# Sum of reciprocals on one core: the last two rows as halves, another order for the last 48 rows, and other load sizes

## Chip, cores and metric

One core of a Trainium2 chip. The metric is the device time of one execution in microseconds (us). The kernel before takes 170.3 us in its fast state and 173.5 in a slow one that a good part of its executions fall into (29 of 64 in the last call); only fast runs are compared. A run counts as fast when it is at most 1.5% above the fastest of its kernel; a few runs of before near 172 us pass by this rule too (see below the table of runs).

## The reference

```python
x = np.abs(np.random.randn(32, 512, 1024)).astype(np.float32) + 1e-6
out = np.sum(1.0 / x, axis=-1)        # [32, 512]
```

That is 67.1 MB to read and 16,384 sums to write: 128 rows of 1024 elements on each of 128 partitions.

## The kernel before

A row's two halves a and b are taken together: 1/a + 1/b = (a + b) / (a b). The product a b comes from GpSimd (P in the list), or from VectorE (W from SBUF; V with one half copied by TensorE, C). ScalarE makes its reciprocal as exp(-ln(.)) (L, then E). VectorE multiplies and reduces it (R): over 1024 elements against both halves of the row, or over 512 where TensorE has added the halves into PSUM (S, two matmuls). The order of all this is a fixed list; each engine runs its own entries in order (the traces show all 153 operations of VectorE before the change, and all 151 after it, in the list's order by kind) and waits on semaphores. D8 loads the next eight rows into a ring of 40. P4+2 is two rows from row 4 on; the number behind @ is a PSUM bank or, for L, a slot for products. The traces record each of these matmuls as two, so a row's S shows there as four (268 records for 67 S in before's).

```python
    F = 128; R = 40; NP = 22          # rows, ring, slots for products
    PLAN = """
        D8 D8 D8 D8 D8 P0+2 C3@7 S2@0 V3 L0+2@0 P2 S3@1 E0+2@6 P4+2 S6@2 L2+2@2 R0 E2+2 R1
        ... (cut)
        S116@2 E112+2@6 R114 W117 L115+2@6 P118 R113 C119@5 E115+2 S119@0 R112 P120
        L117+2@14 V119 E117+2@6 S121@3 W121 R115 L119+3@8 P122 R118 S120@1 R117 E119+3 P123
        R116 S124@4 L122+2@20 P124 R121 R120 E122+2@6 W125 S125@2 R119 L124+2@11 P126 R123
        S126@0 E124+2 P127 R122 L126@3 R125 S127@1 E126 R124 L127@16 R126 E127 R127
    """.split()
    ...
            elif op == "R":
                other = ps[:, bank[r], :]
                if r in halves:                       # S has added the halves
                    row = prod[:, p, :]
                else:
                    row = ring[:, r % R, :].rearrange("p (h e) -> p h e", h=2)
                    other = other.unsqueeze(1).to_broadcast([P, 2, H])
                inst = nc.vector.tensor_tensor_reduce(
                    out=row, in0=row, in1=other, scale=S, scalar=0.0,
                    op0=mult, op1=add, accum_out=sums[:, r : r + 1])
```

## Time and profile before

| | before |
|---|---|
| first three times | 170.43, 170.23, 173.33 us |
| profiled run | 174.07 us, span 172.1 us, slow |
| data moved by DMA until | about 160.5 us, at some 425 GB/s |
| last load complete (all 16 increments) | 162.08 us |
| VectorE's last sum | 169.61 us |

The span runs from the first to the last instruction. An engine's busy time counts; what decides is the chain of waits that reaches the end. The lines are in the prediction below.

### The profile page before, as it was taken

Reading aid. Unit: us, or ns where it says so; the run is one execution under the profiler, and the core shown is the slowest. Engines: PE = TensorE matmul, PEld = TensorE weight load, DVE = VectorE, ACT = ScalarE, POOL = GpSimd, SP = SyncE. Lnnn points to the kernel's source line nnn. Section 1 sums busy time; section 2 is a strip of 40 time slices with the busy share of each in tenths; the row PEclk is TensorE's granted clock in tenths of the full one; section 3 lists DMA queues with packets and bytes.
Section 4 is the critical chain, followed back from the end, with each engine's and each line's share of the span. In section 5 each row is a group of like instructions: output and inputs, shape, how many; then the busy total and the mean of one; then the engine's idle time right before and its main releaser. Section 6 shows DMA issues by size and latency. Waiting matters only on the chain.

```text
span 172.1 us, 1294 instructions
## 1 busy us (share of the span) xinstructions
PE 136.1 (79%) x300; PEld 57.1 (33%) x300; DVE 131.9 (77%) x281; ACT 131.1 (76%) x133; POOL 124.6 (72%) x73
## 2 busy tenths in 40 slices
PE   0007999696987949489695999589999999997892
PEld 0003444242423424143342443134444343442440
DVE  0001786868689685868868689998699999999994
ACT  2002969979696977949698799989689796996992
POOL 1007969696997959589696999789739749977800
PEclk9999999999999999999999999969999999999999
DMA  6999999999999999999999999999999999999200
GB/s 198 427 442 411 449 411 449 411 449 427 449 421 396 427 434 430 421 442 411 434 428 430 404 426 447 424 426 429 427 416 423 429 424 413 410 410 409 101 0 15
DMA packets 4758, 67.24 MB, mean 391 GB/s; under 512 B 528, under 2 KB 656, under 8 KB 1808
## 3 DMA queue, kind: packets, MB, share of 16 engines
q1 hardware_dynamic: 4752, 67.18, 92.5%
q8 instruction: 2, 0.03, 0.1%
q14 instruction: 4, 0.03, 0.0%
HBM read 67.11 MB, written 0.07 MB: 390 GB/s over the span
## 4 chain that ended last, share of the span: by engine, by line
DMA 52%; DVE 29%; PE 6%; ACT 5%; issue 3%; POOL 3%; SPq 0%; ACTq 0%; POOLq 0%; DVEq 0%
DMA ring<-in_x_dram 52%; DVE ring L232 14%; DVE prod L232 8%; DVE prod L191 5%; PE ps L200 5%; POOL prod L175 3%; ACT ps L219 2%; ACT prod L210 2%; PE ps L185 1%; ACT prod L219 1%; DVE sums L232 1%; SPq L165 0%; ACTq L210 0%; POOLq L175 0%; DVEq L286 0%
## 5 line engine op out<-in xcount | busy, mean ns | idle before, releaser
L175 POOL TENSOR_TENSOR prod<-ring 128x1024 f32<-128x1024 f32 (+1 forms) x67 | 123.9, 1880 | 38.3 <-DMA ring<-in_x_dram 37.2
L200 PE MATMUL ps<-ring,ident 128*128 128x512 f32 x268 | 121.6, 606 | 5.2 <-DVE sums L232 2.6
L210 ACT ACTIVATE prod<-prod 128x1024 f32<-128x1024 f32 (+2 forms) x66 | 67.3, 1020 | 32.9 <-POOL prod L175 28.1
L232 DVE CUSTOM_DVE_ANT_1 ring<-ring,ps 128x1024 f32<-128x1024 f32 x61 | 72.1, 1216 | 17.9 <-ACT ps L219 17.9
L200 PEld LDWEIGHTS ps<-ring,ident 128*128 128x128 f32 x268 | 51.5, 194 | 73.7 <-issue 60.1
L232 DVE CUSTOM_DVE_ANT_0 prod<-prod,ps 128x512 f32<-128x512 f32 x67 | 43.4, 682 | 2.1 <-PE ps L200 1.6
L185 PE MATMUL ps<-ring,ident 128*128 128x512 f32 x32 | 17.9, 647 | 27.4 <-DMA ring<-in_x_dram 27.4
L219 ACT ACTIVATE prod<-prod 128x1024 f32<-128x1024 f32 (+2 forms) x34 | 35.4, 1042 | 0.9
L219 ACT ACTIVATE ps<-prod 128x1024 f32<-128x1024 f32 (+2 forms) x32 | 31.6, 986 | 3.2 <-DVE sums L232 2.4
L191 DVE TENSOR_TENSOR prod<-ring,ps 128x512 f32<-128x512 f32 x16 | 11.0, 685 | 17.7 <-PE ps L185 17.7
L185 PEld LDWEIGHTS ps<-ring,ident 128*128 128x128 f32 x32 | 5.6, 196 | 37.0 <-DMA ring<-in_x_dram 16.8
L232 DVE DVE_READ_ACCUMULATOR2_ANT sums<- 128x1 f32 x128 | 10.5, 82 | 0.0
L191 DVE TENSOR_TENSOR prod<-ring 128x512 f32<-128x512 f32 x9 | 10.2, 1154 | 0.0
L77 ACT ACT_TABLE_LOAD x1 | 1.3, 1283 | 0.7 <-PEq L275 0.7
masks.py:197 POOL MEMSET ident<- 128x128 f32 x1 | 0.2, 204 | 0.3 <-POOLq L275 0.3
masks.py:199 POOL TENSOR_SCALAR_AFFINE_SELECT ident<-ident 128x128 f32<-128x128 f32 x1 | 0.3, 292 | 0.1
L275 POOL MEMSET const-float32-0.0<- 128x1 f32 x1 | 0.1, 98 | 0.2 <-issue 0.2
L275 POOL MEMSET const-bfloat16-1.0<- 128x1 bf16 x1 | 0.1, 102 | 0.0
L275 POOL MEMSET const-uint8-127<- 128x1 uint8 x1 | 0.1, 102 | 0.0
L275 POOL MEMSET const-float32-1.0<- 128x1 f32 x1 | 0.1, 98 | 0.0
## 6 DMA issues: line engine op xcount, KB each, us to landing
ring<-in_x_dram SPq DMA_DIRECT2D x9, 4096.0 KB, 38.9
ring<-in_x_dram SPq DMA_DIRECT2D x7, 1536.0 KB, 35.5
ring<-in_x_dram SPq DMA_DIRECT2D x2, 2560.0 KB, 36.8
ring<-in_x_dram SPq DMA_DIRECT2D x9, 512.0 KB, 15.0
ring<-in_x_dram SPq DMA_DIRECT2D x1, 3072.0 KB, 36.4
ring<-in_x_dram SPq DMA_DIRECT2D x3, 1024.0 KB, 29.4
ring<-in_x_dram SPq DMA_DIRECT2D x1, 2048.0 KB, 36.8
out_dram<-sums SPq DMA_DIRECT2D x1, 64.0 KB, 1.5
```

Of the source, the lines that this page charges most:

```text
L77: nc.scalar.add_instruction(mybir.InstLoadActFuncSet(name=nc.get_next_instruction_name(), act_func_set_id=act_sets.index("natural_log_exp_ ...
L175: inst = nc.gpsimd.tensor_tensor(out=prod[:, p : p + m, :], in0=ring[:, a : a + m, :H], in1=ring[:, a : a + m, H:], op=mult,)
L185: inst = nc.tensor.matmul(ps[:, b, :], lhsT=ident, rhs=xs(r, 1), start=True, stop=True)
L191: inst = nc.vector.tensor_tensor(out=prod[:, p, :], in0=xs(r, 0), in1=in1, op=mult)
L200: inst = nc.tensor.matmul(ps[:, b, :], lhsT=ident, rhs=xs(r, h), start=h == 0, stop=h == 1,)
L210: inst = nc.scalar.activation(out=pg, in_=pg, func=Ln, scale=S)
L219: inst = nc.scalar.activation(out=rc, in_=pg, func=Exp, scale=-1.0)
L232: inst = nc.vector.tensor_tensor_reduce(out=row, in0=row, in1=other, scale=S, scalar=0.0, op0=mult, op1=add, accum_out=sums[:, r : r + 1],)
L275: nc = _bacc.Bacc("TRN2", target_bir_lowering=False, num_devices=1)
```

## The change

The intent is a shorter end: finer pieces for the last rows, an order of the last 48 rows found by a search that reckons with the overlap of ScalarE's operations (by before's trace, neighbours start 0.54 us apart where one lasts 0.63), and eight loads of 8 rows ahead of smaller ones. The early rows' order changes in places too.

```diff
+    LAST = F - 2
     PLAN = """  (all new; its end:)
+        ... W124 S123@0 L123@12 R122 L124@15 E123 W125 S125@1 E124@7 P126 R123 L125@16
+        R124 P127 L126@13 E125 P128 S128@0 L127@17 R125 E126@7 P129 S129@2 E127@6 R126
+        L128@18 L129@19 R127 E128 E129 R128 R129
     (loads: 9 of 8 rows and 23 more -> 8 of 8 rows, 25 more, 4 of half a row)
+    def place(r):                  # entries 126 to 129: halves of rows 126 and 127
+        if r < LAST:
+            return r, 0, H
+        q, part = divmod(r - LAST, 2)
+        return LAST + q, part * H, H // 2
 ... (P, C, V, W, S, L, E take width and place from it)
-                    scalar=0.0,
-                    accum_out=sums[:, r : r + 1],
+                    scalar=total if q in summed else 0.0,
+                    accum_out=total,            # total = sums[:, q : q + 1]
```

The second half of such a row starts its sum from the first half's, which it reads as a scalar operand.

More of the change, by code (lines that the diff above doesn't have):

```diff
@@ L25 @@
     NP = 22
+    LAST = F - 2
     S = float(2**17)
     PLAN = """
-        D8 D8 D8 D8 D8 P0+2 C3@7 S2@0 V3 L0+2@0 P2 S3@1 E0+2@6 P4+2 S6@2 L2+2@2 R0 E2+2 R1
-        S7@3 P6+2 L4+2@4 R2 R3 E4+2@6 L6+2@6 R4 P8+2 C11@5 E6+2 R5 D8 S10@0 V11 R6 L8+2@8
-        P10 S11@1 R7 E8+2@6 P12+2 S14@2 L10+2@10 R8 E10+2 R9 S15@3 P14+2 L12+2@12 R10 R11
-        E12+2@6 L14+2@14 R12 P16+2 C19@5 E14+2 R13 D8 S18@0 V19 R14 L16+2@16 P18 S19@1 R15
-        E16+2@6 P20+2 S22@2 L18+2@18 R16 E18+2 R17 S23@3 P22+2 L20+2@20 R18 R19 E20+2@6
@@ L39 @@
-        L22+2@0 R20 P24+2 C27@5 E22+2 R21 D8 S26@0 V27 R22 L24+2@2 P26 S27@1 R23 E24+2@6
-        P28+2 S30@2 L26+2@4 R24 E26+2 R25 S31@3 P30+2 L28+2@6 R26 R27 E28+2@6 L30+2@8 R28
-        E30+2 P32+2 C35@5 R29 D8 S34@0 V35 R30 R31 L32+2@10 P34 S35@1 E32+2@6 P36+2 S38@2
-        L34+2@12 R32 E34+2 R33 S39@3 P38+2 L36+2@14 R34 R35 E36+2@6 L38+2@16 R36 E38+2 R37
-        D6 P40+2 C43@6 R38 S42@0 R39 V43 L40+2@18 P42 S43@1 E40+2@6 P44+2 S46@2 L42+2@20 R40
-        E42+2 R41 D5 S47@3 P46+2 L44+2@0 R42 R43 E44+2@6 L46+2@2 R44 P48+2 C51@5 E46+2 R45
@@ L45 @@
-        D5 S50@0 V51 R46 L48+2@4 P50 S51@1 R47 E48+2@6 P52+2 S54@2 L50+2@6 R48 E50+2 R49
-        S55@3 P54+2 L52+2@8 R50 R51 E52+2@6 L54+2@10 R52 D5 P56+2 C59@5 E54+2 R53 D3 S58@0
-        V59 R54 L56+2@12 P58 S59@1 R55 E56+2@6 P60+2 S62@2 L58+2@14 R56 E58+2 R57 D4 S63@3
-        P62+2 L60+2@16 R58 R59 E60+2@6 L62+2@18 R60 P64+2 C67@5 E62+2 R61 D3 S66@0 V67 R62
-        L64+2@20 P66 S67@1 R63 E64+2@6 P68+2 S70@2 L66+2@0 R64 E66+2 R65 D3 S71@3 P70+2
-        L68+2@2 R66 R67 C75@7 E68+2@5 S74@0 P72+2 V75 L70+2@4 R68 D3 E70+2 S75@1 R69 D3
@@ L51 @@
-        L72+2@6 P74 R70 E72+2@6 R71 P76+2 L74+2@8 R72 S78@2 E74+2 R73 D3 P78+2 S79@3
-        L76+2@10 R74 R75 E76+2@6 C81@5 W82 L78+2@12 P80 R76 D2 L82@14 V81 E78+2 P85+3 S83@0
-        R77 D2 D1 E82@6 L80+2@15 R78 S87@1 R82 E80+2@4 R79 S84@2 L85+3@17 P83+2 R81 R80 D1
-        D1 D1 D1 D1 E85+3 S85@3 D1 P90 L83+2@20 R87 C91@7 R85 P92 L90@0 C88@6 V91 E83+2
-        S92@1 V88 P89 L91@3 R84 E90@7 R83 P94 S86@2 D1 D1 L88+2@4 R90 E91 W93 S93@0 E88+2@6
-        W95 R86 L92+2@1 R89 S91@2 E92+2 P96 R88 C99@7 R92 L94+3@6 P97+2 S99@3 R91 V99
@@ L57 @@
-        E94+3@4 R93 W100 S100@1 L97+2@9 P102 R94 L99+2@14 S101@0 R95 P101 E99+2 R96 S102@2
-        P103 L101+2@11 R100 R99 E97+2@6 P104+2 S105@1 L103@16 R97 E101+2 S104@3 R98
-        L104+2@20 P108 R101 E103@7 S107@4 W106 E104+2 W107 R103 L106+3@17 S106@0 P111 R105
-        E106+3 R104 S108@1 R102 P109+2 L111@13 R106 E111@7 R107 R108 C112@6 L109+2@4 P114
-        R111 S114@0 E109+2@4 V112 P113 L114@0 R109 S115@1 L112+2@1 P115 R110 E114 P116
-        S116@2 E112+2@6 R114 W117 L115+2@6 P118 R113 C119@5 E115+2 S119@0 R112 P120
@@ L63 @@
-        L117+2@14 V119 E117+2@6 S121@3 W121 R115 L119+3@8 P122 R118 S120@1 R117 E119+3 P123
-        R116 S124@4 L122+2@20 P124 R121 R120 E122+2@6 W125 S125@2 R119 L124+2@11 P126 R123
-        S126@0 E124+2 P127 R122 L126@3 R125 S127@1 E126 R124 L127@16 R126 E127 R127
+        D8 D8 D8 D8 D8 P0+2 C3@3 S2@0 V3 P2 L0+2@0 S3@1 E0+2@6 P4+2 S6@2 L2+2@2 R0 E2+2 R1
+        P6+2 L4+2@4 R2 R3 E4+2@6 S7@0 L6+2@6 R4 E6+2 P8+2 C11@3 R5 D8 S10@1 R6 R7 P10 L8+2@8
+        V11 S11@2 E8+2@6 P12+2 S14@0 L10+2@10 R8 E10+2 R9 P14+2 L12+2@12 R10 R11 E12+2@6
@@ new lines @@
+        S15@1 L14+2@14 R12 E14+2 P16+2 C19@3 R13 D8 S18@2 R14 R15 P18 L16+2@16 V19 S19@0
+        E16+2@6 P20+2 S22@1 L18+2@18 R16 E18+2 R17 P22+2 L20+2@20 R18 R19 E20+2@6 S23@2
+        L22+2@0 R20 E22+2 P24+2 C27@3 R21 D8 S26@0 R22 R23 P26 L24+2@2 V27 S27@1 E24+2@6
+        P28+2 S30@2 L26+2@4 R24 E26+2 R25 P30+2 L28+2@6 R26 R27 E28+2@6 S31@0 L30+2@8 R28
+        E30+2 R29 D6 P32+2 C35@3 S34@1 R30 R31 V35 P34 L32+2@10 S35@0 E32+2@6 P36+2 S38@2
+        L34+2@12 R32 E34+2 R33 D5 P38+2 L36+2@14 R34 R35 E36+2@6 S39@1 L38+2@16 R36 E38+2
@@ new lines @@
+        R37 D5 P40+2 C43@3 R38 S42@0 R39 V43 P42 L40+2@18 S43@1 E40+2@6 P44+2 S46@2 L42+2@20
+        R40 E42+2 R41 D3 P46+2 L44+2@0 R42 R43 E44+2@6 S47@0 L46+2@2 R44 E46+2 P48+2 C51@3
+        R45 S50@1 R46 R47 P50 L48+2@4 V51 S51@2 E48+2@6 P52+2 S54@0 L50+2@6 R48 D6 E50+2 R49
+        P54+2 L52+2@8 R50 R51 E52+2@6 S55@1 L54+2@10 R52 E54+2 P56+2 C59@3 R53 D5 S58@2 R54
+        R55 P58 L56+2@12 V59 S59@0 E56+2@6 P60+2 S62@1 L58+2@14 R56 E58+2 R57 D4 D2 P62+2
+        L60+2@16 R58 C67@3 R59 E60+2@6 S63@2 P64+2 V67 L62+2@18 R60 E62+2 S66@0 R61 D4 P66
@@ new lines @@
+        L64+2@20 R62 E64+2@6 R63 P68+2 S67@1 L66+2@0 R64 S70@2 E66+2 R65 D3 P70+2 L68+2@2
+        R66 R67 E68+2@6 S71@0 P72+2 L70+2@4 R68 D2 S74@1 E70+2 R69 D2 P74 L72+2@6 R70 C75@3
+        R71 E72+2@6 P76+2 S75@2 V75 R72 D2 L74+2@8 S78@0 R73 D2 D1 E74+2 P78+2 L76+2@10 R74
+        S80@3 R75 E76+2@6 P80 L78+2@12 S79@1 R76 D1 P81 L80@14 R77 D1 D1 D1 D1 E78+2 P82 E80
+        R78 R80 L81+2@15 R79 E81+2@6 P83 C88@5 R82 S85@0 P84 L83@17 R81 D1 D1 E83@7 P85
+        S86@1 L84@18 R83 D1 E84@6 P86 L85@19 V88 E85 R84 D1 D1 D1 D1 L88@21 P87 L86@20 R85
@@ new lines @@
+        C91@7 E88@6 P93 E86 R88 S90@0 L87@0 P92 E87@5 R86 R87 D1 D1 S89@1 P90 L92+2@1 V91
+        E92+2@5 W89 S91@2 P97 L89+3@3 R92 C94@7 R93 P95 L97@6 E89+3 S97@3 V94 P98 E97 R90
+        S98@4 P99 L98@9 R97 L94+2@7 R91 W96 S96@0 E98 R89 E94+2@6 R98 L96@14 R94 P100 C102@5
+        E96 S101@1 R96 P101 L99+2@10 R95 E99+2@3 P103 V102 L101@12 R99 C106@7 P104 L102+2@15
+        S104@0 R100 E101 P105 L104@13 R101 E102+2@5 S108@2 P107+2 V106 E104 R102 L105+2@17
+        S107@1 R104 E105+2@4 P109+2 R103 L107+2@19 R106 E107+2 R105 P111+2 S112@0 L109+2@0
@@ new lines @@
+        R107 E109+2@6 R108 S111@3 L111+2@2 W114 W113 S113@1 E111+2 R109 P115 L113@21 R111
+        P116 L114+2@4 S116@2 R112 E113 R110 P117 E114+2@5 S117@0 R113 P118 L116+2@6 R115
+        E116+2 P119 R114 L118@8 R116 P120 S120@1 L119@9 R117 E118@7 E119@6 R118 P121 L120@14
+        S121@0 E120 R119 P122 L121@10 S122@2 E121 R120 P123 L122@11 R121 E122 W124 S123@0
+        L123@12 R122 L124@15 E123 W125 S125@1 E124@7 P126 R123 L125@16 R124 P127 L126@13
+        E125 P128 S128@0 L127@17 R125 E126@7 P129 S129@2 E127@6 R126 L128@18 L129@19 R127
@@ L66 @@
+        E128 E129 R128 R129
     """.split()
@@ L104 @@
     pslot = {r + j: b + j for op, r, n, b in ops if op == "L" for j in range(n)}
+    def place(r):
[3 more added lines that the diff above has]
+        return LAST + q, part * H, H // 2
     def xs(r, h):
-        return ring[:, r % R, h * H : (h + 1) * H]
+        q, at, w = place(r)
+        return ring[:, q % R, at + h * w : at + (h + 1) * w]
     loaded = 0
-    bank, copied, halves = {}, {}, set()
+    bank, copied, halves, summed = {}, {}, set(), set()
     history = {}
@@ L149, in note, with rows @@
                 )
-    def rows(r, n):
-        return [("row", q % R) for q in range(r, r + n)]
+    def rows(r, n, h=None):
+        spaces = []
+        for q, at, w in (place(i) for i in range(r, r + n)):
+            end = at + 2 * w
+            if h is not None:
+                at, end = at + h * w, at + (h + 1) * w
+            spaces += [("row", q % R, i) for i in range(at, end, H // 2)]
+        return spaces
     def slots(r, n):
@@ L162 @@
                 while n:
-                    a = r % R
-                    m = min(n, R - a)
+                    q, at, w = place(r)
+                    a = q % R
+                    m = min(n, R - a, LAST - r) if r < LAST else 1
                     inst = nc.sync.dma_start(
-                        out=ring[:, a : a + m, :], in_=x_v[:, r : r + m, :]
+                        out=ring[:, a : a + m, at : at + 2 * w],
+                        in_=x_v[:, q : q + m, at : at + 2 * w],
                     )
@@ L172 @@
                 while n:
-                    a, p = r % R, pslot[r]
+                    q, at, w = place(r)
+                    a, p = q % R, pslot[r]
                     m = min(n, R - a)
                     inst = nc.gpsimd.tensor_tensor(
-                        out=prod[:, p : p + m, :],
-                        in0=ring[:, a : a + m, :H],
-                        in1=ring[:, a : a + m, H:],
+                        out=prod[:, p : p + m, :w],
+                        in0=ring[:, a : a + m, at : at + w],
+                        in1=ring[:, a : a + m, at + w : at + 2 * w],
                         op=mult,
@@ L185 @@
                 inst = nc.tensor.matmul(
-                    ps[:, b, :], lhsT=ident, rhs=xs(r, 1), start=True, stop=True
+                    ps[:, b, : place(r)[2]],
+                    lhsT=ident,
+                    rhs=xs(r, 1),
+                    start=True,
+                    stop=True,
                 )
-                note("PE", inst, rows(r, 1), [("bank", b)])
+                note("PE", inst, rows(r, 1, 1), [("bank", b)])
             elif op in "WV":
-                in1 = xs(r, 1) if op == "W" else ps[:, copied[r], :]
+                w = place(r)[2]
+                in1 = xs(r, 1) if op == "W" else ps[:, copied[r], :w]
                 inst = nc.vector.tensor_tensor(
-                    out=prod[:, p, :], in0=xs(r, 0), in1=in1, op=mult
+                    out=prod[:, p, :w], in0=xs(r, 0), in1=in1, op=mult
                 )
-                other = [("bank", copied[r])] if op == "V" else []
-                note("DVE", inst, rows(r, 1) + other, slots(r, 1))
+                if op == "W":
+                    read = rows(r, 1)
+                else:
+                    read = rows(r, 1, 0) + [("bank", copied[r])]
+                note("DVE", inst, read, slots(r, 1))
             elif op == "S":
@@ L200 @@
                     inst = nc.tensor.matmul(
-                        ps[:, b, :],
+                        ps[:, b, : place(r)[2]],
                         lhsT=ident,
@@ L206 @@
                     )
-                    note("PE", inst, rows(r, 1), [("bank", b)])
+                    note("PE", inst, rows(r, 1, h), [("bank", b)])
             elif op == "L":
-                pg = prod[:, p : p + n, :]
+                pg = prod[:, p : p + n, : place(r)[2]]
                 inst = nc.scalar.activation(out=pg, in_=pg, func=Ln, scale=S)
@@ L212 @@
             elif op == "E":
-                pg = prod[:, p : p + n, :]
+                pg = prod[:, p : p + n, : place(r)[2]]
                 rc = pg
                 if b is not None:
-                    rc = ps[:, b : b + n, :]
+                    rc = ps[:, b : b + n, : place(r)[2]]
                     for j in range(n):
@@ L225 @@
             elif op == "R":
-                other = ps[:, bank[r], :]
+                q, at, w = place(r)
+                other = ps[:, bank[r], :w]
                 if r in halves:
-                    row = prod[:, p, :]
+                    row = prod[:, p, :w]
                 else:
-                    row = ring[:, r % R, :].rearrange("p (h e) -> p h e", h=2)
-                    other = other.unsqueeze(1).to_broadcast([P, 2, H])
+                    row = ring[:, q % R, at : at + 2 * w]
+                    row = row.rearrange("p (h e) -> p h e", h=2)
+                    other = other.unsqueeze(1).to_broadcast([P, 2, w])
+                total = sums[:, q : q + 1]
                 inst = nc.vector.tensor_tensor_reduce(
@@ L236 @@
                     scale=S,
-                    scalar=0.0,
+                    scalar=total if q in summed else 0.0,
                     op0=mult,
                     op1=add,
-                    accum_out=sums[:, r : r + 1],
+                    accum_out=total,
                 )
+                summed.add(q)
                 note(
@@ L247 @@
                 )
-            elif op == "X":
-                row = ring[:, r % R, :]
-                inst = nc.scalar.activation(out=row, in_=row, func=Ln)
-                note("ACT", inst, writes=rows(r, 1))
-                inst = nc.scalar.activation(
-                    out=row,
-                    in_=row,
-                    func=Exp,
-                    scale=-1.0,
-                    accum_out=sums[:, r : r + 1],
-                )
-                note("ACT", inst, writes=rows(r, 1))
         nc.sync.dma_start(out=out_v, in_=sums)
```

## The prediction

> **What bounds the kernel now.** I read the page first for the spread of the load, then the busy time by stretch for the end of the run, then the chain that ended last, and then single durations and the timeline of the last 12 us. The page's strip of 40 slices (4.3 us each):
>
> ```profile
> PEclk9999999999999999999999999969999999999999
> DMA  6999999999999999999999999999999999999200
> GB/s 198 427 442 411 449 411 449 411 449 427 449 421 396 427 434 430 421 442 411 434 428 430 404 426 447 424 426 429 427 416 423 429 424 413 410 410 409 101 0 15
> ```
>
> The DMA engines are full from the second slice to slice 37 and move about 425 GB/s. So the 67.1 MB of x set the first 160 us, whatever the engines do, and only the way from the last load to the end can be shortened. One slice has a reduced TensorE clock. The stretches at the end:
>
> ```profile
> core 0: us, PE busy (x) PEld busy (x) DVE busy (x) ACT busy (x) POOL busy (x), PEclk, DMA share, GB/s
> ...
> 110.00:120.00 10.00, 7.42 (x14) 3.17 (x14) 9.60 (x18) 8.93 (x10) 7.84 (x4) 0.83 0.99 419
> ...
> 130.00:140.00 10.00, 9.65 (x23) 4.07 (x22) 10.00 (x23) 8.75 (x9) 8.41 (x6) 1.00 1.00 422
> 140.00:150.00 10.00, 9.61 (x23) 4.10 (x22) 9.84 (x21) 8.51 (x10) 7.94 (x6) 1.00 1.00 418
> ...
> 160.00:162.00 2.00, 2.00 (x6) 0.89 (x5) 2.00 (x5) 1.97 (x3) 1.18 (x2) 1.00 0.21 84
> 162.00:165.00 3.00, 3.00 (x9) 1.07 (x7) 3.00 (x10) 2.66 (x4) 1.44 (x2) 1.00 0.00 0
> 165.00:170.00 5.00, 3.64 (x9) 1.38 (x8) 4.61 (x12) 3.79 (x6) 0.00 (x0) 1.00 0.00 0
> ```
>
> From 130 us VectorE (DVE) has no gap, and data stop at about 160.5 us, yet VectorE works to 169.6. It carries a backlog of rows. The chain says where that came from:
>
> ```profile
> 112.55 0.14 issue
> 112.68 8.80 PE ps L200 x16
> 121.48 1.73 PE ps L185 x4
> 123.22 0.02 issue
> 123.24 0.69 DVE prod L191
> ```
>
> Sixteen matmuls took 8.80 us, 0.55 each, where the timeline elsewhere starts one every 0.43: in 113 to 117 us the granted clock was 0.57. That cost TensorE about 8.80 - 16 x 0.43 = 1.9 us, and VectorE never caught up. **This profile is a slow run** (174.07 us, against 170.43 and 170.23 of the fast ones), so its 7.5 us after the last load are not what fast runs have. That is the main point of what follows.
>
> [...] 1045 ns for 1024 elements and 620 for 512, and independent neighbours start 0.54 us apart where one lasts 0.63 (below, 167.07 and 167.61). [...] the VectorE product of two SBUF halves (W in the list) takes 1154 ns in the mean, that with a PSUM half (V) 685. [...] In the trace the last load's 16 increments spread from 159.87 to 162.08 us, so its row is usable 1.6 us after the bulk of the data.
>
> **The change part by part.** Durations come from these groups by shape:
>
> ```profile
> L175 POOL TENSOR_TENSOR prod<-ring 128x1024 f32<-128x1024 f32 x34 | 80.6, 2386 | 25.7 <-DMA ring<-in_x_dram 25.7
> L232 DVE CUSTOM_DVE_ANT_1 ring<-ring,ps 128x1024 f32<-128x1024 f32 x61 | 72.1, 1216 | 17.9 <-ACT ps L219 17.9
> L232 DVE CUSTOM_DVE_ANT_0 prod<-prod,ps 128x512 f32<-128x512 f32 x67 | 43.4, 682 | 2.1 <-PE ps L200 1.6
> L175 POOL TENSOR_TENSOR prod<-ring 128x512 f32<-128x512 f32 x32 | 40.9, 1293 | 10.7 <-DMA ring<-in_x_dram 9.6 <-ACT ps L219 1.0
> L191 DVE TENSOR_TENSOR prod<-ring 128x512 f32<-128x512 f32 x9 | 10.2, 1154 | 0.0
> L210 ACT ACTIVATE prod<-prod 128x512 f32<-128x512 f32 x8 | 5.0, 620 | 1.8 <-DVE prod L191 1.8
> ```
>
> In a row back to back they overlap: in the chain a reduction over 1024 elements takes 1.14 us, one over 512 takes 0.60, and a free product 0.60.
>
> *Loads.* By the times at which the loads' semaphores fill, eight rows land every 9.70 us, three every 3.69, one every 1.275: about 1.205 us per row plus 0.07 per load. The list goes from 32 to 37 loads (nine of 8 rows become eight, nine of one row become eleven, and the last two rows become four of half a row). So the last landing moves by 5 x 0.07 = 0.35, from 162.08 to 162.43. Row 125 lands at 159.74 and the halves at 160.41, 161.09, 161.76 and 162.43. Loads stay requested several microseconds ahead, so nothing starves.
>
> *VectorE, rows from 80 on.* Before: 27 short and 21 long reductions, 6 V, 9 W: 27 x 0.60 + 21 x 1.14 + 6 x 0.60 + 9 x 1.154 = 54.1 us. After: 23 short, 23 long, two over 512 and two over 256 elements (estimate 0.35 from the slope), 5 V, 6 W: 13.8 + 26.2 + 1.2 + 0.7 + 3.0 + 6.9 = 51.8. That is 2.3 us less, but in 60 us of loads, so only a backlog would turn it into time.
>
> *The end before, in a fast run.* Two floors. Last row: landed 162.08, product to 163.43, logarithm 0.61, exponential 0.63, reduction 0.69 and 0.1 of hand-over: 165.5. VectorE: W121 cannot start before row 121 is there, 154.50, and behind it come W125, nine short and four long reductions: 2 x 0.60 + 9 x 0.605 + 4 x 1.14 = 11.2, so 165.8 with 0.1 of waking. The slow profile ended VectorE at 169.6; the fast runs are 174.07 - 170.43 = 3.64 shorter, so about 166.0. **Fast runs already sit on the floor of 165.8**: the backlog that the profile shows is that of a slow run.
>
> *The end after.* VectorE floor: W125 from 159.84, then R123 0.605, R124 1.14, R125 0.605, R126 and R127 0.60 each, R128 and R129 0.35 each: with W125's own 0.60 that is 4.85, so 164.7. Last half: GpSimd takes about 0.75 for half a row (line through 1284 at 512 and 2386 at 1024 elements). It runs P126 from 160.5 to 161.25, P127 to 162.0, P128 to 162.75, and P129, whose half landed at 162.43, to 163.5. Then L129, E128 and E129 of 0.40 each, the two exponentials overlapping by 0.1 beside each other, to 164.6, then R129 0.35 and a hand-over: about 165.1. Against 166.0 that is **0.85 us less**.
>
> How the tail of before looked in the profile, ScalarE:
>
> ```profile
> 167.07 0.63 ACT L219 ACTIVATE prod<-prod 128x512 f32<-128x512 f32 x1
> 167.61 0.61 ACT L210 ACTIVATE prod<-prod 128x512 f32<-128x512 f32 x1
> 168.25 0.63 ACT L219 ACTIVATE prod<-prod 128x512 f32<-128x512 f32 x1
> ```
>
> *ScalarE and list.* Single rows replace pairs and threes from row 80 (50 operations of 512 or 256 elements instead of 16). Each costs 0.2 more than its share of a pair, and interleaving rows gives back 0.09 per neighbour. Sum for rows from 80: 2 x (21 x 0.615 + 4 x 0.40 + 11 x 1.045 + 1.48) = 55 us, less some 4 of overlap, in 60 us of loads: it fits, with little to spare. The early rows' new order and the loads' sizes there lie under the full DMA.
>
> Sum: 170.43 - 0.85 = 169.6 us.
>
> **Rivals.** (1) *The backlog is real in fast runs too.* Then the 2.3 us less of VectorE work and the finer end are worth up to the distance from 169.6 to 165.1, and the time is 166 to 168. For it: the unbroken VectorE busy time. Against it: fast runs are 3.6 us shorter than the profiled one, and the backlog follows a clock dip. (2) *A new wait takes the gain.* VectorE runs in order, and W124 and W125 stand in its list waiting for loads [...]. The last two reductions also read the sum that the one before them writes. ScalarE's single operations leave it little slack. Then 170.4 to 171.2. (3) *DMA loses more on 2 KB pieces than on 4 KB ones*: if a half takes 0.75 instead of 0.67, 0.3 us of the gain goes, 169.9. (4) *Transfers hide it all*: the early part of the change should do nothing, as its rows wait for data.
>
> **Range and chances.** From the step of 0.85 less, plus or minus rival 2 or half of rival 1: 168.4 to 170.8. Faster by over 2% needs under 167.0, another 2.6 us, more than the whole VectorE saving, or rival 1 in full: 4%. Slower by over 2% needs 3.4 us of new waits: 3%. Within 2%: 93%.
>
> **What would show it.** In the profile after: the last load's semaphore full about 0.35 us later than before, if the DMA runs alike; half-row products near 0.75 us and half-row ScalarE operations near 0.40; six W with a mean near or under 1.15; the output issued under 3.2 us after the last landing. It is wrong if VectorE is still busy without a gap for over 4 us after the last landing in a run with full clock (rival 1 or 2), or if the stretch from 150 us moves under 395 GB/s (rival 3). If the profile after falls in the fast state, it says little against a slow one: then the timed runs decide.

The 1045 and 620 ns are ScalarE's operations over 1024 and 512 elements (L210 in before's profile). The last row's product on GpSimd started at 162.15 us, 0.07 after the last of the 16 increments.

## The result, and the profile after

A ratio is the mean time of one kernel's fast runs over that of the other's in the same rounds, so not quite the ratio of the medians quoted. After: 170.06 us median (169.95 to 170.29, four runs), ratio to before 0.9986, interval 0.9962 to 1.001. Two later comparisons gave 0.9981 (0.9972 to 0.9991) and 0.9970 (0.9950 to 0.9989). So it is about 0.3 us faster in the fast state, not 0.85.

The stretches of the changed kernel's end, busy time by engine (columns as in the prediction):

```profile
160.00:162.00 2.00, 2.00 (x7) 1.01 (x6) 1.75 (x4) 2.00 (x5) 1.86 (x3) 1.00 0.17 65
162.00:165.00 3.00, 1.61 (x8) 1.08 (x6) 2.47 (x10) 2.09 (x7) 0.93 (x2) 1.00 0.00 0
165.00:170.00 5.00, 0.00 (x0) 0.00 (x0) 0.49 (x2) 0.00 (x0) 0.00 (x0) 0.60 0.06 16
```

No engine is full after 162 us, and VectorE ends at 165.65; the last load was complete at 161.88. Nothing has a backlog, and still 3.77 us pass. VectorE's timeline there:

```profile
163.29 0.08 DVE L264 DVE_READ_ACCUMULATOR2_ANT sums<- 128x1 f32 x1
163.53 0.75 DVE L264 CUSTOM_DVE_ANT_1 ring<-ring,ps,sums 128x512 f32<-128x512 f32 x1 [0.15 <-DVE sums L264]
164.20 0.08 DVE L264 DVE_READ_ACCUMULATOR2_ANT sums<- 128x1 f32 x1
164.20 0.42 DVE L264 CUSTOM_DVE_ANT_0 prod<-prod,ps 128x256 f32<-128x256 f32 x1
164.54 0.08 DVE L264 DVE_READ_ACCUMULATOR2_ANT sums<- 128x1 f32 x1
165.17 0.48 DVE L264 CUSTOM_DVE_ANT_0 prod<-prod,ps,sums 128x256 f32<-128x256 f32 x1 [0.54 <-DVE sums L264]
165.57 0.08 DVE L264 DVE_READ_ACCUMULATOR2_ANT sums<- 128x1 f32 x1
```

These are R127, R128 and R129 with the reads that store their sums. R127 and R129 take a sum as operand (the name `sums` behind the arrow), and VectorE waits for itself: 0.15 and 0.54 us (0.15 to 0.16 and 0.54 to 0.55 in two more profiles of this kernel and in a_pause). Why the second wait is the longer is open: R127 starts 0.10 us after VectorE's own semaphore instruction, R129 0.46 us after it, though ScalarE's last exponential had ended at 164.20. The new short operations, from the groups by shape:

```profile
L217 DVE TENSOR_TENSOR prod<-ring 128x512 f32<-128x512 f32 x6 | 4.0, 688 | 0.4 <-DMA ring<-in_x_dram 0.4
L196 POOL TENSOR_TENSOR prod<-ring 128x256 f32<-128x256 f32 x4 | 2.8, 726 | 1.9 <-DVE prod L217 1.9
L239 ACT ACTIVATE prod<-prod 128x256 f32<-128x256 f32 x4 | 1.5, 404 | 0.0
```

They cost what was reckoned (0.75 and 0.40). The six W take 688 ns, where before's nine take 1154 in its slow profile and 824 in its fast one (below). They hardly meet GpSimd's products any more: one starts in the last 0.12 us of such a product (691 ns), the others beside none. In before's slow profile the five W that start inside one take 1.00 to 1.85 us, the other four 0.68 to 0.69.

### The profile page after: what moved, and what is told of

Read it like the earlier page. It is cut to its first block, busy times and chain, and to the rows that moved or that the text cites. A ratio compares the mean times of both kernels' runs of the same rounds, so it can differ in the third digit from the quotient of the medians.

```text
span 168.3 us, 1338 instructions
## 1 busy us (share of the span) xinstructions
PE 131.5 (78%) x290; PEld 54.2 (32%) x290; DVE 128.3 (76%) x281; ACT 133.3 (79%) x155; POOL 129.4 (77%) x82
## 4 chain that ended last, share of the span: by engine, by line
DMA 72%; DVE 8%; POOL 6%; PE 4%; issue 4%; ACT 3%; SPq 0%; DVEq 0%; POOLq 0%
DMA ring<-in_x_dram 72%; POOL prod L196 6%; DVE ring L264 4%; PE ps L229 4%; DVE prod L264 2%; ACT ps L248 2%; ACT prod L239 1%; DVE prod L217 1%; DVE sums L264 0%; SPq L184 0%; DVEq L264 0%; POOLq L196 0%; DVEq L307 0%
## 5 line engine op out<-in xcount | busy, mean ns | idle before, releaser
L196 POOL TENSOR_TENSOR prod<-ring 128x1024 f32<-128x1024 f32 (+2 forms) x76 | 128.7, 1726 | 33.0 <-DMA ring<-in_x_dram 30.6
L229 PE MATMUL ps<-ring,ident 128*128 128x512 f32 (+1 forms) x260 | 117.0, 598 | 10.1 <-DVE sums L264 8.9
L239 ACT ACTIVATE prod<-prod 128x1024 f32<-128x1024 f32 (+2 forms) x77 | 68.7, 902 | 28.3 <-POOL prod L196 27.6
L264 DVE CUSTOM_DVE_ANT_1 ring<-ring,ps 128x1024 f32<-128x1024 f32 x64 | 75.4, 1209 | 19.4 <-ACT ps L248 19.0
L229 PEld LDWEIGHTS ps<-ring,ident 128*128 128x128 f32 x260 | 49.4, 193 | 76.4 <-issue 54.6
L264 DVE CUSTOM_DVE_ANT_0 prod<-prod,ps 128x512 f32<-128x512 f32 x64 | 41.5, 678 | 0.8 <-ACT prod L248 0.4
L248 ACT ACTIVATE prod<-prod 128x1024 f32<-128x1024 f32 (+3 forms) x40 | 35.0, 881 | 0.9
L206 PE MATMUL ps<-ring,ident 128*128 128x512 f32 x30 | 17.5, 667 | 22.0 <-DMA ring<-in_x_dram 21.6
L248 ACT ACTIVATE ps<-prod 128x1024 f32<-128x1024 f32 (+2 forms) x37 | 33.5, 908 | 1.0
L217 DVE TENSOR_TENSOR prod<-ring,ps 128x512 f32<-128x512 f32 x15 | 10.2, 683 | 16.1 <-PE ps L206 15.9
L206 PEld LDWEIGHTS ps<-ring,ident 128*128 128x128 f32 x30 | 4.8, 196 | 32.6 <-issue 14.4
L217 DVE TENSOR_TENSOR prod<-ring 128x512 f32<-128x512 f32 x6 | 4.0, 688 | 0.4 <-DMA ring<-in_x_dram 0.4
```

What stands on the lines that cost most here:

```text
L196: inst = nc.gpsimd.tensor_tensor(out=prod[:, p : p + m, :w], in0=ring[:, a : a + m, at : at + w], in1=ring[:, a : a + m, at + w : at + 2 * w],
L206: inst = nc.tensor.matmul(ps[:, b, : place(r)[2]], lhsT=ident, rhs=xs(r, 1), start=True, stop=True,)
L217: inst = nc.vector.tensor_tensor(out=prod[:, p, :w], in0=xs(r, 0), in1=in1, op=mult)
L229: inst = nc.tensor.matmul(ps[:, b, : place(r)[2]], lhsT=ident, rhs=xs(r, h), start=h == 0, stop=h == 1,)
L239: inst = nc.scalar.activation(out=pg, in_=pg, func=Ln, scale=S)
L248: inst = nc.scalar.activation(out=rc, in_=pg, func=Exp, scale=-1.0)
```

## The experiments

Theory A: the sum of a second half must wait until the first half's sum is stored, and this chain on VectorE ate the gain. Rivals: the end hangs on ScalarE or GpSimd (B), the halves as such carry the gain (C), reading a sum costs at any distance (D). The first call had b_again to a_whole, the second a_nochain2 to b_halved, the third a_whole3 to a_inter_few, the last the rest.

| run | median us of all runs | fast runs | ratio to before (interval) |
|---|---|---|---|
| b_again | 173.50 | 1 of 6 | none given |
| a_again | 170.09 | 16 of 16 | 0.9981 (0.9972 to 0.9991) |
| a_nochain (wrong on purpose) | 168.41 | 6 of 6 | 0.9881 (0.9859 to 0.9904) |
| a_nochain2 (wrong on purpose) | 169.41 | 6 of 6 | 0.9913 (0.9867 to 0.9960) |
| a_inter | 169.92 | 6 of 6 | 0.9940 (0.9893 to 0.9986) |
| a_whole2 | 171.18 | 6 of 6 | 1.0016 (0.9970 to 1.0063) |
| b_halved | 174.96 | 2 of 6 | 1.0063 (0.9970 to 1.0157) |
| a_whole3 | 170.74 | 22 of 22 | 1.0009 (0.9991 to 1.0026) |
| a_inter38 | 169.51 | 15 of 15 | 0.9940 (0.9917 to 0.9963) |
| a_loads34 | 176.73 | 6 of 6 | 1.0342 (1.0294 to 1.0391) |
| a_inter_few | 175.37 | 6 of 6 | 1.0283 (1.0235 to 1.0331) |
| b_again2 | 170.54 | 14 of 20 | 1.0000 (0.9970 to 1.0030) |
| a_pause | 170.46 | 22 of 22 | 0.9985 (0.9969 to 1.0002) |
| a_again2 | 170.05 | 22 of 22 | 0.9970 (0.9950 to 0.9989) |
| a_inter38b | 169.47 | 11 of 11 | 0.9928 (0.9904 to 0.9953) |

The runs of before near 172 us that count as fast (2 of 7 in the second call, 5 of 30 in the third, 3 of 35 in the last, none in the first) pull these ratios down. Worked out again without them, a_inter has 0.9970, a_inter38b 0.9943, a_again2 0.9980.

**The same two kernels again** (no edit).

> The kernel before, unchanged, to get a profile of it in the fast state and the noise of the comparison. Theory of the record: VectorE ends at about 166.0 us and the last load is complete at 162.0, so fast runs sit on their floor. Rival: the last load lands earlier in fast runs (161.5 or less) and some backlog of VectorE stays. Ratio to before 1.000 within 0.002.

> The changed kernel, unchanged, beside the same runs of before as the others of this call: ratio 0.9986 within 0.002 if the first comparison holds; 0.995 if the forecast of 0.85 us less was right and the first four runs were unlucky.

a_again repeated the result; b_again's profile was slow again, with the half clock at 113 us (a granted clock of 0.83 over 110 to 120 us, as in before, whose trace has 0.50 from 113.42 to 116.84).

**Without the chain.** Both kernels give each half a sum column of its own:

```diff
-    sums = pool.tile([P, F], f32)
+    sums = pool.tile([P, COLS], f32)          # COLS = F + 2
-                total = sums[:, q : q + 1]
+                total = sums[:, r : r + 1]
-                    scalar=total if q in summed else 0.0,
+                    scalar=0.0,
-        nc.sync.dma_start(out=out_v, in_=sums)
+        nc.sync.dma_start(out=out_v, in_=sums[:, :F])      # a_nochain
+        nc.sync.dma_start(out=out_v, in_=sums[:, 2:COLS])  # a_nochain2
```

> The changed kernel, but each half of the last two rows has a sum column of its own, so no reduction reads the sum that the one before it wrote. Wrong on purpose: rows 126 and 127 of each partition get one half's sum alone. Theory A (chained sums cost the gain: 0.15 + 0.07 us at R127 and 0.54 + 0.06 at R129): VectorE ends about 0.7 to 0.9 us earlier than in the changed kernel, 169.2 us, ratio to before 0.994. Rival B (the end hangs on ScalarE or GpSimd and the wait lies beside it): within 0.1 us of the changed kernel.

> As a_nochain, but the output waits for all four half sums (in a_nochain it took columns 0 to 127 and left 0.6 us before the last two reductions ended, so its time flattered). Wrong on purpose: the columns put out are 2 to 129. Theory A (chained sums cost about 0.95 us on VectorE, from R126's start to the last read of a sum 2.97 against 2.01 us): 169.1 us, ratio to before 0.9925. Rival B': the gain of a_nochain was only the early output: 170.0.

a_nochain gained more than theory A allows: its output was issued at 163.81 us, before the last two reductions had ended. That was a fault of the experiment. a_nochain2 mends it: 169.41, where A said 169.1 and B' 170.0. On VectorE, from R126's start to the last stored sum, 2.97 us became 2.01. So B falls.

**The halves in another order, correct.**

```diff
-        q, part = divmod(r - LAST, 2)
+        part, q = divmod(r - LAST, 2)
```

The entries are now 126a, 127a, 126b, 127b, so one other reduction stands between writing and reading a sum. One of the four loads moved behind R87, which frees its place.

> The changed kernel, correct, with the four halves in another order: first halves of rows 126 and 127, then their second halves, so that a reduction reads a sum that the one before the last wrote. Theory A: most of the 0.95 us comes back, 169.2 to 169.5 us, ratio 0.993 to 0.995. Rival D (it is the read of a sum as scalar operand itself that costs, at any distance): still 170.0.

VectorE's end in a_inter, by the timeline:

```profile
163.90 0.48 DVE L264 CUSTOM_DVE_ANT_0 prod<-prod,ps,sums 128x256 f32<-128x256 f32 x1
164.31 0.08 DVE L264 DVE_READ_ACCUMULATOR2_ANT sums<- 128x1 f32 x1
164.31 0.48 DVE L264 CUSTOM_DVE_ANT_0 prod<-prod,ps,sums 128x256 f32<-128x256 f32 x1
164.71 0.08 DVE L264 DVE_READ_ACCUMULATOR2_ANT sums<- 128x1 f32 x1
```

Both second halves read a sum and neither waits. The last load was complete at 161.88 as in the changed kernel, and VectorE ended at 164.79 instead of 165.65: 0.86 us, as theory A said. D falls: from R126's start it is 2.13 us, 0.12 above the version that reads no sum. But the time fell by 0.14 only (medians on two chips; the two profiled runs, 170.09 and 169.76 us, differ by 0.33).

**Where the other 0.7 us went.** The first step is at the very end. After issuing the output, SyncE goes through some waits and joins the other engines. In a_inter its trace (the packed one, as no view lists these instructions) has a pause of 0.41 us between its 79th and 80th recorded instruction, where such neighbours stand 0.04 to 0.06 apart; a_whole2 has 0.41 at the same place. In the changed kernel the 79th and 80th enclose the wait for the output itself (1.18 us), so a pause there would be hidden. a_inter's stream is one instruction shorter. Two runs test it. a_inter38 (and a_inter38b, the same file) splits one load of two rows, so the stream grows by two:

```diff
-        ... D2 L74+2@8 S78@0 R73 D2 D1 E74+2 ...
+        ... D2 L74+2@8 S78@0 R73 D1 D1 D1 E74+2 ...      (and a_inter's edit)
```

a_pause loads the second half of each of the two rows first, which needs one wait less and shortens the changed kernel's stream by one; its work is otherwise the same, and it is correct:

```diff
-        return LAST + q, part * H, H // 2
+        return LAST + q, (1 - part) * H, H // 2
```

> a_inter with its last load of two rows split into two loads, 38 loads in all. In a_inter VectorE ended 0.86 us earlier than in the changed kernel, the time fell by 0.14 only. Its SyncE pauses 0.41 us between its 79th and 80th instruction, and there the output is already complete; in the changed kernel the same place in the stream falls into the wait for the output. Theory P (a pause at a fixed place of the instruction stream): one more load moves the place into the wait; the span shrinks by 0.37 less 0.07 for the load: 169.6 us. Rival: the pause stays behind the output or another comes: 169.9 to 170.0.

> The changed kernel with the second half of each of the two last rows loaded first. The work is the same, instruction by instruction; one load needs one semaphore less, so SyncE's stream is one instruction shorter (86 for 87) and the place of its pause falls just behind the completed output. Theory P: VectorE ends as in the changed kernel, 165.6 to 165.8, and the time is 0.35 us longer: 170.4. Rival: 170.05 as the changed kernel.

> The changed kernel as it is, on the same chip as a_pause and a_inter38b: 170.05 to 170.10 us, ratio to before 0.998.

> a_inter38 once more, the candidate that beats both kernels, on the same chip as the changed kernel: 169.5 us, 0.55 less than a_again2, ratio to before 0.994 to 0.995. Rival: the first call had a quick chip, and the two are within 0.2 us.

On one chip: a_again2 170.10 in the mean, a_pause 170.47 (its VectorE ended at 165.49, and the pause of 0.41 stood behind the output), a_inter38b 169.47 (the pause of 0.43 stood ahead of the wait for the output, inside the transfer). The times are as expected, though a_pause's VectorE ended a little before the 165.6 of its expectation and a_inter38b's ratio fell below its 0.994. So the pause is worth about 0.37 us when it is exposed. That it belongs to a place in SyncE's stream is shown by seven traces at four lengths of the stream (82, 84, 86 and 88 instructions), all with the pause between the 79th and the 80th; what SyncE does there is open. It had taken about 0.4 of a_inter's gain. In the two profiled runs the account closes: SyncE passes the wait for the output at 166.57 instead of 167.34, 0.77 earlier (the transfer took 0.09 longer), and needs 1.37 us instead of 0.97 behind it, so the span is 0.37 shorter. That the medians differ by 0.14 only has no run of its own; profiled single runs of one kernel differ by as much as 0.4 (168.3 and 168.7 us of span for the changed one).

a_inter38 beats both kernels: 0.63 us less than the changed one on the same chip, 0.7% less than before (0.6% without the runs near 172 us).

**The last rows whole, with the new list.** a_whole was spoilt: the two loads left out were the wrong ones, so a row was overwritten before it was read (215.83 us, wrong result); nothing follows from it. a_whole2 and a_whole3 are correct. They differ in whether TensorE adds the halves of row 126:

```diff
-    LAST = F - 2
+    LAST = F
 ... (two of the four D1 taken out; the end of the list:)
-        P128 S128@0 L127@17 R125 E126@7 P129 S129@2 E127@6 R126 L128@18 L129@19 R127 E128 E129 R128 R129
+        S126@0 E125 L126@13 R125 S127@2 E126 L127@17 R126 E127 R127        # a_whole2
+        L126@13 E125 R125 E126@6 S127@0 L127@17 R126 E127 R127            # a_whole3
```

> The changed list and loads, but the last two rows whole, as before. Theory A: a whole last row needs 1.28 + 0.61 + 0.63 + 0.69 us behind its landing at 161.85, so VectorE ends at about 165.3 to 165.5, which is the same as or a little better than the changed kernel's 165.65: the halves gain nothing as they are. Rival C (the halves are what makes the changed kernel the faster): 0.5 to 1.2 us slower than it, above 170.5.

> The changed list and loads with whole last rows, as a_whole should have been: there the two loads left out were the wrong ones, so row 127 was loaded before row 87 had been read, and the result was wrong and the run meaningless. Theory A: VectorE ends at 165.3 to 165.5, so 169.8 to 170.1 us: the halves gain nothing as they are. Rival C (the halves make the changed kernel what it is): above 170.6.

> The changed list with whole last rows once more; in a_whole2 both whole rows were summed on TensorE, whose 20 matmuls in a row ended only at 165.25 us and set the end. Here row 126 goes without TensorE (a long reduction), row 127 with it, as of the four halves two go each way. If TensorE's queue alone made whole rows slower: VectorE ends at 165.2 to 165.5 and the time is 170.0 to 170.4 (with the pause of SyncE of 0.37 us that a_whole2 and a_inter show after the output). If halving the last row's latency is worth something by itself: VectorE ends at 165.9 or later, above 170.5.

a_whole2's expectation missed. Its last line on the timeline of VectorE says why:

```profile
165.40 0.69 DVE L263 CUSTOM_DVE_ANT_0 prod<-prod,ps 128x512 f32<-128x512 f32 x1 [1.02 <-PE ps L228]
```

R127 waited for TensorE, whose queue of twenty recorded matmuls ended that late: S126 and S127 over 512 elements had replaced S128 and S129 over 256. That was a choice of the experiment. In a_whole3 row 126 goes without TensorE: VectorE ends at 165.68, as in the changed kernel (165.65), and the 170.76 us of its fast runs' mean holds an exposed pause of 0.41. Less that pause it is 170.4. This expectation missed too: VectorE's end lies between its two cases, and the time is where rival C put it. But in the profiles the output is complete at 167.27, in the changed kernel at 167.34, and SyncE then needs 1.61 us instead of 0.97: the pause, and waits that it passed before the output's end in the changed kernel. So the time lost lies wholly behind the output, and on VectorE rival C falls for the change as it stands: the halves gain nothing there, and a_nochain2 and a_inter show that the chain takes what they save. With the chain loosened (a_inter) they are worth 0.86 to 0.89 us there.

**The old list with halves.** The end of before's list, halves spliced in, in the changed kernel's code:

```diff
-        W125 S125@2 R119 L124+2@11 P126 R123 S126@0 E124+2 P127 R122 L126@3 R125 S127@1 E126 R124 L127@16 R126 E127 R127
+        W125 S125@2 R119 L124+2@11 P126 R123 E124+2 P127 R122 L126@3 R125 P128 S128@0 L127@13 E126@7 R124 P129
+        S129@1 E127@6 R126 L128@18 L129@19 R127 E128 E129 R128 R129
```

> The list and loads of before, with only the last two rows as halves. Theory A (VectorE's backlog from W121 on is the floor of before, and the halves add about 0.7 us of reductions and 0.9 us of waits behind it): slower than before by 0.7 to 1.6 us, 171.0 to 171.9 in the fast state. Rival C (halves shorten the last row and that is what counts): 0.5 us or more faster than before.

Only two runs were fast, 171.61 and 172.36, beside fast runs of before with a median of 170.44. The direction is that of theory A, but the interval reaches below 1, so this alone decides nothing. No profile of it is fast.

**Larger loads.** The changed list with nine loads of 8 rows and larger ones behind them, each issued as soon as its rows are free; a_inter_few does the like with a_inter and 33 loads.

```diff
-    8 x D8, D6, D5, D5, D3, D6, D5, D4, D2, D4, D3, D2 D2 D2 D2, 11 x D1, 4 halves      (37 loads)
+    9 x D8, D6, D5, D5, D5, D3, D4, D3 D3 D3 D3 D3, D2 D2, 7 x D1, 4 halves             (34, a_loads34)
+    9 x D8, D6, D5 D5 D5 D5 D5, D4, D3 D3, D2 D2, 9 x D1, 4 halves                      (33, a_inter_few)
```

In both, one of the loads of 5 rows crosses the end of the ring and is cut in two, as one of before's is; the 34 of a_loads34 counts it, the 33 of a_inter_few does not.

> The changed kernel with nine loads of 8 rows and before's sizes behind them: 34 loads for 37, each issued as soon as its rows are free. If the size of a load costs 0.07 us each, the last half lands 0.2 us earlier and VectorE ends 0.1 to 0.2 us earlier; if the end hangs on TensorE and VectorE alone, no change of VectorE's end (165.65). By the count of its waits SyncE's pause falls behind the output: time 169.9 to 170.4.

> The candidate: a_inter with 33 loads (nine of 8 rows, larger ones after them), so that the last half lands about 0.2 us earlier and SyncE's stream ends before its 79th instruction. Expected 169.2 to 169.6 us, ratio to before 0.993 to 0.996. If bursts of larger loads make rows wait: 170 or more.

Both are over 5 us slower than the kernels that they were made from. Of what was expected, only a_inter_few's other case (170 or more, if bursts make rows wait) has the direction, and neither has the size. Their last loads landed as early as ever (161.54 and 161.66). The stretches of a_loads34, then the same of the changed kernel:

```profile
90.00:100.00 10.00, 7.87 (x15) 3.44 (x16) 7.23 (x16) 7.68 (x8) 8.55 (x5) 0.83 0.97 412
...
120.00:130.00 10.00, 10.00 (x20) 4.19 (x19) 8.08 (x16) 7.25 (x10) 7.03 (x6) 0.81 1.00 424
...
160.00:165.00 5.00, 3.73 (x9) 1.67 (x10) 5.00 (x14) 4.78 (x9) 2.54 (x4) 1.00 0.03 13
```

```profile
90.00:100.00 10.00, 9.59 (x21) 3.93 (x22) 9.07 (x22) 9.84 (x11) 10.00 (x6) 1.00 0.99 424
...
120.00:130.00 10.00, 10.00 (x25) 4.49 (x24) 9.43 (x20) 9.45 (x12) 8.17 (x7) 1.00 1.01 424
```

The data flow alike (the last two columns), but in 90 to 130 us VectorE does 32.2 us of work (with the two stretches not shown) instead of 36.4, and then has no gap from 140 to 165. Rows that arrive in larger bursts leave the list, tuned to other arrivals, waiting: ahead of its V, VectorE waited 21.0 us in all for TensorE's copies, 15.9 in the changed kernel, and row 72 lands at 99.31 instead of 96.09. Half clocks at 93 and 117 us (granted 0.83 over 90 to 100 us, 0.85 and 0.81 over the two stretches from 110 us) come on top, and the six W of a_loads34 take 1014 ns in the mean again, and no run tells the two shares apart.

**Before in the fast state.**

> The kernel before once more, for a profile in the fast state. Theory of the record: VectorE ends at 165.8 to 166.1 us with the last landing at 161.5 to 162.1, and no half clock near 113 us. Rival: VectorE ends there too, but a half clock lies at 113 us as in the slow ones, so the slow state has another cause.

Its profile was fast at last (170.75 us). The end of the chain that ended last, VectorE's last reduction on the timeline, and the group of the nine W:

```profile
158.31 7.15 PE ps L200 x16
...
165.59 0.69 DVE prod L232
165.59 0.69 DVE L232 CUSTOM_DVE_ANT_0 prod<-prod,ps 128x512 f32<-128x512 f32 x1 [0.41 <-PE ps L200]
L191 DVE TENSOR_TENSOR prod<-ring 128x512 f32<-128x512 f32 x9 | 7.3, 824 | 0.2 <-DMA ring<-in_x_dram 0.2
```

VectorE ended at 166.28 in a run 0.4 us longer than the usual fast one, so at about 165.9 in those, by this estimate; the prediction had inferred 166.0. No half clock lay near 113 us (one lay at 73.4 to 76.8). TensorE's timeline at that place, before in the fast state, then the changed kernel in a_again2:

```profile
112.50 7.11 PE L200 MATMUL ps<-ring,ident 128*128 128x512 f32 x16 [2.60 <-DMA ring<-in_x_dram]
```

```profile
115.09 5.76 PE L229 MATMUL ps<-ring,ident 128*128 128x512 f32 x8
```

The sixteen matmuls that took 8.80 us in the slow profile take 7.11 here. a_again2 had a half clock from 112.6 to 119.5 us, its eight matmuls took 5.76 us (3.60 at full clock), and the run still took 170.46. In a_again one of half that length lay there and the span was 168.30, as without it. So a half clock that lies there goes with before's slow runs and cost the new list 0.4 us at most in these runs. The traces show a second thing that goes with it: in the slow profiles (before, b_again, and b_halved) four W behind it take 1.0 to 1.8 us beside GpSimd's products, where in the fast one all behind 113 us take 0.68 to 0.75. Over the nine W that is 3.0 us, about what the slow state costs. No run tests whether the half clock brings it about. In the last call 29 of 64 runs of before were slow and none of 55 of the three kernels with the new list; a_whole3 (22 of 22 fast) shows that this is not owed to the halves. Each stretch at half clock (a_whole and the starts and ends of the runs left out) lasted 3.41 or 6.83 us, around the end of a gap of TensorE of 2.3 to 3.0 us, in the two kernels with larger loads 3.5 and 4.8. The gap alone does not decide: in the first profile of the changed kernel, in a_nochain and in a_inter38 one of 3.0 us left the clock full, and in before's fast profile one of 2.6.

## Why the prediction was right or wrong

- *Only the end can be shortened; fast runs of before sit near 166.0.* Right: about 165.9. What sets it was named wrongly: not VectorE's work from W121 on, but TensorE's sixteen last recorded matmuls (S124 to S127, from row 124's landing on), for which R127 waited 0.41 us. That the floor of 165.8 fits is luck.
- *Five more loads move the last landing by 0.35 us.* Wrong: 161.88 and 161.99 in two profiles of the changed kernel, 161.99 in the fast one of before. The half loads of 256 KB took 0.64 us each (about 410 GB/s), not the 0.75 of rival 3, and half of the 1.275 that a row's 512 KB took before. By this term the end should have come 0.55 earlier than forecast.
- *Cost of the new short operations, six cheaper W, 2.3 us less VectorE work.* The short operations are right. The W were priced from a slow profile: between the fast profiles VectorE's busy time fell by 1.2 us (129.5 to 128.3), not 2.3, as before's W take 824 ns there and not 1154. The saved work did not become time, as there was no backlog in fast runs; rival 1 is refuted.
- **The step that failed is the sum "R126 and R127 0.60 each, R128 and R129 0.35 each" and the "hand-over" behind E129.** It charged nothing for the read of a sum just written. Rival 2 named that read and did not price it. From R126's start to the last stored sum the forecast makes 1.90 us; measured are 2.97, and 2.01 where no sum is read (a_nochain2). R127 waits 0.15 and R129 0.54, the two take 0.07 and 0.06 longer (748 ns for 681, 481 for 418), and they lose their overlap with the operation in front (0.08 us where no sum is waited for); taking the chain apart gave 0.86 us back on VectorE (a_inter). From the last landing to VectorE's end it was 3.77 us, forecast 2.67; a_inter needs 2.91. Of the forecast's terms, P129 took 1.05 us for 1.07, L129 to E129 1.27 for 1.1, and R129 with its hand-over 1.45 for 0.5.
- *From VectorE's end to the time.* The prediction took it as fixed. With SyncE's pause it is not: it moves by 0.37 us with the length of SyncE's stream (a_pause). In the changed kernel its place falls into the wait for the output (1.18 us between the two instructions), which would hide it.
- *The early rows' order and the loads' sizes there lie under the full DMA.* Not so in general: a_loads34 lost over 5 us with the DMA as full as ever (a share of 0.97 to 1.02 from 90 to 130 us).

Sum: the end came 0.55 earlier by the landing and 1.10 later by the path behind it, of which the chain is 0.86 (a_inter) to 0.96 (a_nochain2). So 0.3 us remained of the forecast 0.85.

## What to carry to other kernels

When a sum is cut into pieces, let a piece not read the accumulator of the piece just before it: put another operation between, which here cost one line and one moved load and gave 0.86 us of VectorE's end (in time 0.63 on one chip, with SyncE's pause hidden). A list of work tuned in a fixed order, as here, belongs to its load sizes; change one, and try tuning the other again (both kernels with larger loads lost over 5 us, half clocks included). Before adding up the end of a kernel, get a profile in the state of the runs that are to be forecast, and when an engine's end moves and the time does not, look at the instructions behind the output.
